# Half of the low part of each weight tile by an adding DMA in place of VectorE, in a one-layer fp32 encoder

## The chip, the cores and the metric

The kernel runs on one core of a Trainium2 chip. The metric is the device time of one execution in microseconds. The core has TensorE (matrix products, into the accumulators called PSUM), VectorE and ScalarE (elementwise work), GpSimd (called POOL in the profile), and 16 DMA engines, to which transfers are sent from the queues of SP, ScalarE or POOL. Each of these engines works through its own list of instructions in order, and they wait for each other by semaphores.

## What is computed

One layer of an encoder on 256 tokens of width 2048, all in fp32: a norm, one input projection to 10,240 columns (queries, keys and values of two kinds of attention, and gates), differential attention and neighbourhood attention, two branch projections that are gated and added, an output projection, a norm with a residual, and a squared-ReLU MLP of width 8192 with a norm and a residual.

```python
h = rms_norm(x, norm_mix_pre[l])
proj = jnp.einsum('bsd,dc->bsc', h, w_in[l])
qa, ka, va, qn, kn, vn, gates = jnp.split(proj, split_at, axis=-1)
...
mixed = (g_a * jnp.einsum('bsc,cd->bsd', oa, w_branch_a[l])
         + g_b * jnp.einsum('bsc,cd->bsd', on, w_branch_b[l]))
y = jnp.einsum('bsd,de->bse', mixed, w_out[l])
x = x + rms_norm(y, norm_mix_post[l])
h = rms_norm(x, norm_mlp_pre[l])
u = jnp.square(jax.nn.relu(jnp.einsum('bsd,df->bsf', h, w_up[l])))
x = x + rms_norm(jnp.einsum('bsf,fd->bsd', u, w_down[l]), norm_mlp_post[l])
```

The weights have 62.9 million numbers (252 MB). Each is read once.

## The kernel before

**Two parts for each number.** TensorE multiplies in a format called float32r, which keeps fewer bits than fp32. So each weight and each activation is given as the sum of a high part (the value cast to float32r) and a low part (value minus high part, again float32r), and a product is made of three: high by high, low by high, high by low.

**Tiles.** Weights come in tiles of 1 MiB, 128 partitions by 2048 numbers. For all projections but the last this is four row blocks of 128 by 512 columns; for the down projection (`dweight`, L750) one row block by 2048 columns. `load` (L94) sends the DMA of a tile into a buffer `raw` from SP's queue (L98). `split` (L101) makes the two parts in the buffers `hi` and `lo`. It does so in two pieces of 128 by 1024 (the very first tile: four pieces): for each, ScalarE casts raw to hi (L115) and VectorE subtracts hi from raw into lo (L116). The pool `wp` has three buffers each of raw, hi and lo, so a load waits until the split of the tile three before is done with its raw buffer, and a split waits until TensorE has used the tile three before.

**Who uses them.** `wgroup` (L183) keeps weights stationary: for four blocks of 128 columns and four row blocks, one product of the high part with both parts of the activations (512 columns, L191) and one of the low part with the high part of the activations (256 columns, L192). `agroup` (L220) and the down projection (`dmm`, L772) keep activations stationary and make three products of 512 columns (L229 to L231, L777 to L779). In `wgroup` and `agroup` the second piece of a tile is its third and fourth row block; in the down projection it is columns 1024 to 2047, used from the third of eight accumulators on.

**Order.** Input projection (20 groups of four tiles, with the stages of the attention heads traced between the tiles by `advance`, L172), in the last part with the branch projections (two tiles a group) among the gates; then the output projection (16 tiles), the MLP's up projection (64), and the down projection (64). The names in the profile follow the projections: `qa`, `ka`, `va`, `qn`, `kn`, `vn` for query, key and value; `ga`, `gb` gates; `ba`, `bb` branches; `y` output; `u` up; `d` down. `u_w`, `u_h`, `u_l` are raw, high and low part of a tile of the up projection; `u_p` its accumulators, `acc` those of the down projection. Besides the tiles, VectorE and ScalarE empty the accumulators (`halves`, L251), and do the norms' and the attention's elementwise work.

**Other lines named below.** `inv_rms` (L81) computes a norm's factor: its power runs on POOL (L88), the only work that POOL has once the constants are made. `residual_parts` (L653) adds the residual (L657) and transposes for the MLP (L664). A chore (L323, L336) prepares the position bias by way of DRAM. The order of each engine's instructions is set by a planner that lays out the traced program in simulated time.

Of the kernel before, what the change touches and what calls it, by code (L numbers as in the profile page):

```python
# [38 lines left out]
def encoder_layer(ctx: ExitStack, tc: tile.TileContext, a, out):  # L39
# [30 lines left out]
        return tmp.tile([P, 2, T], F32, tag="t2k", name=n, bufs=7)  # L70

    def along_tokens(r, b, name):
        """r [P tokens, token tile] as a row of all tokens, on all partitions."""
        ps = bank(f"{name}_p")
        for t in range(2):
            dg = t1k(f"{name}_d{t}")
            nc.vector.tensor_scalar_mul(dg[:, :P], ident, r[:, t : t + 1])
            nc.tensor.matmul(ps[:, t * P : (t + 1) * P], ones, dg[:, :P], start=True, stop=True)
        nc.scalar.copy(b, ps[:, :T])

    def inv_rms(ss, n, name, r=None):  # L81
        """(ss / n + eps) ** -0.5, per partition."""
        w = ss.shape[1]
        ms_ = small(w, f"{name}_m")
        nc.vector.tensor_scalar(ms_, ss, 1.0 / n, EPS, op0=ALU.mult, op1=ALU.add)  # L85
        if r is None:
            r = small(w, f"{name}_r")
        nc.gpsimd.tensor_tensor(r, ms_, expo[:, :w], op=ALU.pow)  # L88
        return r

# [1 line left out]
    last_load = [None]  # L92

    def load(src, k0, nk, c0, cw, name):  # L94
        """Rows k0*128.. of a weight: [P, nk, cw]."""
        raw = wp.tile([P, nk, cw], F32, tag="raw", name=f"{name}_w")
        view = src[k0 * P : (k0 + nk) * P, c0 : c0 + cw].rearrange("(k p) c -> p k c", p=P)
        last_load[0] = nc.sync.dma_start(raw, view).ins  # L98
        return raw

    def split(raw, name, pieces=2, after=()):  # L101
        """Two float32r parts whose sum is raw. after[s] are instructions that go ahead of piece s."""
        _, nk, cw = raw.shape
        hi = wp.tile([P, nk, cw], F32R, tag="hi", name=f"{name}_h")
        lo = wp.tile([P, nk, cw], F32R, tag="lo", name=f"{name}_l")
        for s in range(pieces):
            part = (
                (slice(None), slice(s * nk // pieces, (s + 1) * nk // pieces))
                if nk > 1
                else (slice(None), slice(None), slice(s * cw // pieces, (s + 1) * cw // pieces))  # L110
            )
            with ExitStack() as order:
                for ins in after[s] if after else ():
                    order.enter_context(tc.issue_after(ins))
                nc.scalar.copy(hi[part], raw[part])  # L115
                nc.vector.tensor_sub(lo[part], raw[part], hi[part].bitcast(F32))  # L116
        return hi, lo

    def weight(src, k0, nk, c0, cw, name, after=()):
        return split(load(src, k0, nk, c0, cw, name), name, after=after)  # L120

# [1 line left out]
    g_pre = const.tile([P, KD], F32, name="g_pre")  # L123
    nc.scalar.dma_start(g_pre, a["g_mix_pre"])
    ident = const.tile([P, P], F32, name="ident")
# [44 lines left out]
    pace = [1]  # L170

    def advance(n):  # L172
        """Trace the next n stages of the attention heads that wait for their turn, and one chore."""
        if chores:
            with tc.issue_after(last_load[0]):
                chores.pop(0)()
        for _ in range(n):
            if pending:
                g = pending.pop(0)
                if next(g, None):  # L180
                    pending.append(g)

    def wgroup(src, c0, act, nk, evac, name, first=(), hook=None, mid=None, after={}, k_first=False, inner=None):  # L183
        """out^T of 512 columns: weights stationary. act(k) is [P, hi 256 | lo 256]."""
        ps = [bank(f"{name}_p{b}", True) for b in range(4)]

        def product(b, k, w):
            hi, lo = w
            cs = slice(b * P, (b + 1) * P)
            mv = act(k)  # L190
            nc.tensor.matmul(ps[b], hi[:, k % 4, cs], mv, start=(k == 0), stop=False)  # L191
            nc.tensor.matmul(  # L192
                ps[b][:, :T], lo[:, k % 4, cs], mv[:, :T], start=False, stop=(k == nk - 1)
            )

        for ch in range(nk // 4):
            ks = range(ch * 4, ch * 4 + 4)
            order = hook(ch) if hook else None
            advance(pace[0])
            if ch < len(first):  # L200
                w = split(first[ch], f"{name}_{ch}", 4 if ch == 0 else 2, order)
            else:
                w = weight(src, ch * 4, 4, c0, 512, f"{name}_{ch}", [after.get(ch, ())] * 2)
            if k_first and ch == 0:
                last = None
                for k in ks:
                    last = (inner(k) if inner else None) or last
                    with tc.issue_after(last) if last else nullcontext():
                        for b in range(4):
                            product(b, k, w)  # L210
            else:
                for b in range(4):
                    for k in ks:
                        product(b, k, w)
                    if ch == nk // 4 - 1:
                        if mid and b == 0:
                            mid()
                        evac(b, ps[b])

    def agroup(src, c0, stat, nk, evac, name, tail=1, between=None):  # L220
        """out of 512 columns: activations stationary. stat(k, t) is (hi, lo) of [P, 128].
        The last ``tail`` chunks go token tile by token tile; between(i) may trace instructions
        ahead of the i-th of the second tile's products there and returns the last of them."""
        ps = [bank(f"{name}_p{t}", True) for t in range(2)]

        def product(t, k, w):
            hi, lo = w
            sh, sl = stat(k, t)
            nc.tensor.matmul(ps[t], sh, hi[:, k % 4], start=(k == 0), stop=False)  # L229
            nc.tensor.matmul(ps[t], sh, lo[:, k % 4], start=False, stop=False)  # L230
            nc.tensor.matmul(ps[t], sl, hi[:, k % 4], start=False, stop=(k == nk - 1))  # L231

        n = nk // 4
        for ch in range(n - tail):
            advance(pace[0])
            w = weight(src, ch * 4, 4, c0, 512, f"{name}_{ch}")
            for t in range(2):
                for k in range(ch * 4, ch * 4 + 4):
                    product(t, k, w)
        advance(pace[0])  # L240
        ws = [weight(src, ch * 4, 4, c0, 512, f"{name}_{ch}") for ch in range(n - tail, n)]
        for t in range(2):
            last = None
            for i, k in enumerate(range((n - tail) * 4, nk)):
                if t and between:
                    last = between(i) or last
                with tc.issue_after(last) if last else nullcontext():
                    product(t, k, ws[i // 4])
            evac(t, ps[t])

    def halves(ps, name):  # L251
        """The sum of the two halves of a bank, in SBUF."""
        r = t1k(f"{name}_r")
        nc.scalar.copy(r, ps[:, T:])
        s = t1k(f"{name}_s")
        nc.vector.tensor_add(s, ps[:, :T], r)
        return s

# [1 line left out]
    hT = [page([P, 2, 512], F32R, f"hT{i}") for i in range(8)]  # L260

    def x_parts(i):
        """The transpose of four tiles of x times the gain, in two parts [P, hi | lo]."""
        acts = []
        for k in range(i * 4, i * 4 + 4):
            pt = bank(f"hT_t{k}")
# [50 lines left out]
        )  # L317
        nc.vector.tensor_scalar_mul(subs, subln, 1.0 - LAMBDA_INIT)

    # Position bias: row (h, i) of rpbp holds the bias of row offset i - 3 at column offsets  # L320
    # -63..63. Each is written 64 times at a pitch of 127 and read at a pitch of 126.
    def skew_write(h):
        nc.sync.dma_start(  # L323
            skew[h * NR : (h + 1) * NR].rearrange("r c j -> c r j"),
# [38 lines left out]
            x_squares(3)  # L363
        return [[]] + [acts[i : i + 1] for i in range(3)] if ch == 0 else None

# [1 line left out]
    oT = {}  # L367

    def parts(dst, at, src):
# [2 lines left out]
        nc.vector.tensor_sub(lo[at], src, hi[at].bitcast(F32))  # L372

    def product3(ps, stat, s_at, mov, m_at, start, stop):
        """ps (+)= stat^T @ mov, each given in two parts."""
        for i, (sp, mp) in enumerate(((0, 0), (0, 1), (1, 0))):
            nc.tensor.matmul(
                ps, stat[sp][s_at], mov[mp][m_at], start=start and i == 0, stop=stop and i == 2
# [38 lines left out]
        return evac  # L417

    def p_transposed(p, name):
        """[P queries, (t, keys)] -> [P keys, (key tile, queries)]"""  # L420
        pt = bank(f"{name}_pt")
        for kt in range(2):
            for t in range(2):
# [167 lines left out]
                chores += [lambda: None] * 10 + [partial(position_bias, j) for j in range(2, 4)]  # L591
    pace[0] = 2

# [1 line left out]
    mT = []  # L595
    for cg in range(4):
        gate = []
# [22 lines left out]
        nc.vector.tensor_sub(ml, gate[0], mh.bitcast(F32))  # L620
        mT.append((mh, ml))

# [1 line left out]
    def mstat(k, t):  # L624
        mh, ml = mT[k // 4]
        return mh[:, k % 4, t * P : (t + 1) * P], ml[:, k % 4, t * P : (t + 1) * P]
# [87 lines left out]
    tail = [residual_parts(1, 0)]  # L714
    after = {1: tail[0][1:]}

# [1 line left out]
    def first_up_inner(k):  # L718
        if k == 1:
            tail.append(residual_parts(1, 1, tail[0][2]))  # L720
# [101 lines left out]
def _host_arrays(inputs):  # L822
# [15 lines left out]
        "lam_k1": f["lam_k1"],  # L838
        "lam_q2": f["lam_q2"],
        "lam_k2": f["lam_k2"],  # L840
        # row offsets -3..3 are the ones that four rows reach
        "rpbp": np.pad(f["na_rpb"][0][:, 4:11], ((0, 0), (0, 0), (48, 48))),
    }
    inv = np.float32(1.0) / (
# [28 lines left out]
```

## Time and profile before

| | us |
|---|---|
| median of three runs | 1397.35 |
| lowest and highest | 1396.53, 1397.74 |
| span of the profiled execution, first to last instruction | 1394.5 |
| TensorE / VectorE / ScalarE / POOL busy in it | 1374.6 / 835.8 / 668.7 / 7.9 |
| load queue, share of the 16 DMA engines | 57.3% |

Durations in the profile come from the one profiled execution. A busy TensorE is not one at its peak, since its products overlap and their ends are modelled. Shares of the DMA engines are the time that packets took, over 16 engines and the span; in short windows they can exceed 1 where packets overlap. The mean granted clock of TensorE in this execution is 0.995 of full speed. In rows such as `L115 ACT CAST d_h<-d_w ... x128 | 128.3, 1052 | 191.1 <-PE acc L779 187.5`, the first pair is busy time in us and the mean of one in ns, and what follows is the engine's idle time just before and what ended it.

### The profile page before, as it was taken

What the parts mean: (1) busy time and instruction counts of PE and PEld (TensorE: products, weight loads), DVE (VectorE), ACT (ScalarE), POOL (GpSimd) and SP (SyncE); (2) the same over time, 40 slices, a digit from 0 to 9 for tenths busy, and PEclk for the clock granted to TensorE, in tenths of its full rate; (3) what the DMA queues carried; (4) which work ended last, traced back from release to release, by engine and by line L of the source; (5) the groups of instructions that cost most, each with busy time, mean ns of one, the idle gap of its engine ahead of it and who ended that gap; (6) DMA issues with size and microseconds to landing.
All of it is one profiled execution on the core that took longest, in us unless ns stands there. A gap on an engine that the chain in (4) does not pass through costs nothing.

```text
span 1394.5 us, 17896 instructions
## 1 busy us (share of the span) xinstructions
PE 1374.6 (99%) x7240; PEld 1177.8 (84%) x7240; DVE 835.8 (60%) x1155; ACT 668.7 (48%) x1023; POOL 7.9 (1%) x19
## 2 busy tenths in 40 slices
PE   7999999999999999999899999999999999999997
PEld 6888888888888888888788888888888888888886
DVE  6868866676656565654755555555575554444445
ACT  7554554545444445543744444444464543334332
POOL 0000000000000000000000000000000000000000
PEclk9999999999999999999999999999999999999999
DMA  9674755564555555675455565656555556555551
GB/s 317 202 214 154 202 177 173 171 191 155 165 205 182 203 181 183 203 279 184 149 182 181 182 193 170 211 170 200 189 196 185 203 186 227 195 187 205 181 199 73
DMA packets 117490, 265.16 MB, mean 190 GB/s; under 512 B 15008, under 2 KB 16288, under 8 KB 109216
## 3 DMA queue, kind: packets, MB, share of 16 engines
q1 hardware_dynamic: 117264, 264.03, 57.3%
q8 instruction: 56, 0.92, 0.3%
q14 instruction: 26, 0.21, 0.0%
q10 hardware_dynamic: 144, 0.01, 0.0%
HBM read 261.92 MB, written 3.92 MB: 191 GB/s over the span
## 4 chain that ended last, share of the span: by engine, by line
PE 98%; DVE 1%; DMA 0%; ACT 0%; SPq 0%; issue 0%; DVEq 0%; POOLq 0%; POOL 0%; ACTq 0%
PE u_p L191 17%; PE u_p L192 9%; PE acc L779 8%; PE acc L778 8%; PE acc L777 8%; PE gb_p L191 4%; PE ga_p L191 4%; PE qa_p L191 2%; PE gb_p L192 2%; PE ga_p L192 2%; PE ka_p L191 2%; PE qn_p L191 2%; PE bb_p L191 2%; PE ba_p L191 2%; PE kn_p L191 2%; PE y_p L229 2%
## 5 line engine op out<-in xcount | busy, mean ns | idle before, releaser
L191 PE MATMUL u_p<-h2T,u_h 128*128 128x512 f32 x1024 | 359.9, 398 | 0.5 <-DVE r_m L85 0.5
L192 PE MATMUL u_p<-h2T,u_l 128*128 128x256 f32 x1024 | 284.3, 280 | 0.0
L116 DVE TENSOR_TENSOR d_l<-d_w,d_h 128x1024 fp32r<-128x1024 f32 x128 | 151.1, 1221 | 164.2 <-ACT d_h L115 163.7
L116 DVE TENSOR_TENSOR u_l<-u_w,u_h 128x1024 fp32r<-128x1024 f32 x128 | 151.1, 1222 | 146.0 <-ACT u_h L115 144.7
L191 PEld LDWEIGHTS u_p<-h2T,u_h 128*128 128x128 f32 x1024 | 192.0, 189 | 45.5 <-DVE r_m L85 0.9
L115 ACT CAST d_h<-d_w 128x1024 fp32r<-128x1024 f32 x128 | 128.3, 1052 | 191.1 <-PE acc L779 187.5
L778 PE MATMUL acc<-d_l,uh 128*128 128x512 f32 x512 | 199.0, 389 | 0.0
L779 PE MATMUL acc<-d_h,ul 128*128 128x512 f32 x512 | 198.9, 389 | 0.0
L777 PE MATMUL acc<-d_h,uh 128*128 128x512 f32 x512 | 198.2, 389 | 0.0
L192 PEld LDWEIGHTS u_p<-h2T,u_l 128*128 128x128 f32 x1024 | 193.8, 189 | 1.3
L115 ACT CAST u_h<-u_w 128x1024 fp32r<-128x1024 f32 x128 | 128.0, 1049 | 123.9 <-PE u_p L191 62.5
L778 PEld LDWEIGHTS acc<-d_l,uh 128*128 128x128 f32 x512 | 96.1, 188 | 20.1
L777 PEld LDWEIGHTS acc<-d_h,uh 128*128 128x128 f32 x512 | 96.1, 188 | 20.0
L779 PEld LDWEIGHTS acc<-d_h,ul 128*128 128x128 f32 x512 | 96.1, 188 | 19.8
L191 PE MATMUL gb_p<-hT,gb_h 128*128 128x512 f32 x256 | 90.4, 398 | 0.0
L191 PE MATMUL ga_p<-hT,ga_h 128*128 128x512 f32 x256 | 90.0, 397 | 0.0
L192 PE MATMUL gb_p<-hT,gb_l 128*128 128x256 f32 x256 | 71.4, 281 | 0.0
L192 PE MATMUL ga_p<-hT,ga_l 128*128 128x256 f32 x256 | 70.3, 280 | 0.0
L191 PEld LDWEIGHTS gb_p<-hT,gb_h 128*128 128x128 f32 x256 | 47.9, 188 | 11.5
L116 DVE TENSOR_TENSOR gb_l<-gb_w,gb_h 128x1024 fp32r<-128x1024 f32 x32 | 37.8, 1221 | 31.1 <-ACT gb_h L115 31.1
L191 PEld LDWEIGHTS ga_p<-hT,ga_h 128*128 128x128 f32 x256 | 47.4, 188 | 10.5
L116 DVE TENSOR_TENSOR y_l<-y_w,y_h 128x1024 fp32r<-128x1024 f32 x32 | 37.9, 1222 | 27.8 <-ACT y_h L115 27.8
(213 smaller groups left out, 2348.1 us busy)
## 6 DMA issues: line engine op xcount, KB each, us to landing
u_w<-in_w_up SPq DMA_DIRECT2D x64, 1024.0 KB, 5.4
d_w<-in_w_down SPq DMA_DIRECT2D x64, 1024.0 KB, 4.9
ga_w<-in_w_in SPq DMA_DIRECT2D x16, 1024.0 KB, 5.2
gb_w<-in_w_in SPq DMA_DIRECT2D x16, 1024.0 KB, 5.2
y_w<-in_w_out SPq DMA_DIRECT2D x16, 1024.0 KB, 5.1
ka_w<-in_w_in SPq DMA_DIRECT2D x8, 1024.0 KB, 6.1
va_w<-in_w_in SPq DMA_DIRECT2D x8, 1024.0 KB, 5.2
qn_w<-in_w_in SPq DMA_DIRECT2D x8, 1024.0 KB, 5.1
```

Source lines behind the costliest of these rows:

```text
L115: nc.scalar.copy(hi[part], raw[part])
L116: nc.vector.tensor_sub(lo[part], raw[part], hi[part].bitcast(F32))
L191: nc.tensor.matmul(ps[b], hi[:, k % 4, cs], mv, start=(k == 0), stop=False)
L192: nc.tensor.matmul(ps[b][:, :T], lo[:, k % 4, cs], mv[:, :T], start=False, stop=(k == nk - 1))
L229: nc.tensor.matmul(ps[t], sh, hi[:, k % 4], start=(k == 0), stop=False)
L777: nc.tensor.matmul(acc[t][c], uh[:, k % 4, ts_], hi[:, 0, cs], start=(k == 0), stop=False)
L778: nc.tensor.matmul(acc[t][c], uh[:, k % 4, ts_], lo[:, 0, cs], start=False, stop=False)
L779: nc.tensor.matmul(acc[t][c], ul[:, k % 4, ts_], hi[:, 0, cs], start=False, stop=(k == NK - 1))
```

## The change

For the second of the two pieces of each tile, VectorE's subtraction is replaced. ScalarE writes the negative high part into lo, and an adding DMA, issued from POOL's queue, adds raw onto it in place. The first piece, and the four pieces of the very first tile, are made as before. The other lines of the diff are docstrings and comments that fall away.

```diff
                 nc.scalar.copy(hi[part], raw[part])
-                nc.vector.tensor_sub(lo[part], raw[part], hi[part].bitcast(F32))
+                if s == 1 and pieces == 2:
+                    nc.scalar.mul(lo[part], hi[part].bitcast(F32), -1.0)
+                    nc.gpsimd.dma_start(lo[part], raw[part], accum_op=ALU.add)
+                else:
+                    nc.vector.tensor_sub(lo[part], raw[part], hi[part].bitcast(F32))
```

## The prediction, made before the changed kernel was run

> **What bounds the kernel now.** I read the page first (busy time, chain, DMA queues), then the list of waits, then the order of time in the last stage, and last the windows.
>
> ```profile
> span 1394.5 us, 17896 instructions
> ...
> PE 1374.6 (99%) x7240; PEld 1177.8 (84%) x7240; DVE 835.8 (60%) x1155; ACT 668.7 (48%) x1023; POOL 7.9 (1%) x19
> ...
> q1 hardware_dynamic: 117264, 264.03, 57.3%
> ...
> PE 98%; DVE 1%; DMA 0%; ACT 0%; SPq 0%; issue 0%; DVEq 0%; POOLq 0%; POOL 0%; ACTq 0%
> ```
>
> TensorE is busy 99% of the span, and the chain that ended last is 98% TensorE. VectorE, which the change relieves, works 60% of the span and holds 1% of the chain. All that any relief could bring is the time without TensorE: 1394.5 - 1374.6 = 19.9 us, and most of that is start and end. The DMA engines, which the change loads, are at 57.3% with 264.03 MB.
>
> How a tile moves is seen best in the down projection, in order of time on ScalarE, VectorE and the load queue:
>
> ```profile
> 1200.64 2.01 ACT L115 CAST d_h<-d_w 128x1024 fp32r<-128x1024 f32 x2 [3.43 <-PE acc L779]
> 1206.08 2.00 ACT L115 CAST d_h<-d_w 128x1024 fp32r<-128x1024 f32 x2 [3.43 <-PE acc L779]
> ...
> 1201.73 2.36 DVE L116 TENSOR_TENSOR d_l<-d_w,d_h 128x1024 fp32r<-128x1024 f32 x2 [3.07 <-ACT d_h L115]
> ...
> 1204.11 5.77 SPq L98 DMA_DIRECT2D d_w<-in_w_down  x2
> ...
> d_w<-in_w_down SPq DMA_DIRECT2D x64, 1024.0 KB, 4.9
> ```
>
> One tile takes 1206.08 - 1200.64 = 5.44 us. ScalarE casts only when TensorE has given back a buffer (that of three tiles before), VectorE follows and is done at 1204.09, and at 1204.11 SP sends the load into the raw buffer that VectorE has just finished with. The load lands 4.9 us later, at about 1209. That buffer's next cast comes three tiles after the one at 1200.64, at 1217, so 8 us are to spare. The split itself is ready at 1204.1 for products that begin two tiles after the cast, at about 1211.5. So every producer has room, and TensorE alone sets the pace.
>
> **The change part by part.** A tile is 1 MiB; there are 80 of the input projection, 16 of the branches, 16 of the output, 64 up and 64 down, 240 in all. The first is cut in four and keeps VectorE, so 239 tiles are changed.
>
> ```profile
> L116 DVE TENSOR_TENSOR d_l<-d_w,d_h 128x1024 fp32r<-128x1024 f32 x128 | 151.1, 1221 | 164.2 <-ACT d_h L115 163.7
> ...
> L115 ACT CAST d_h<-d_w 128x1024 fp32r<-128x1024 f32 x128 | 128.3, 1052 | 191.1 <-PE acc L779 187.5
> ...
> 680.00:1030.00 350.00, 350.00 (x2009) 305.28 (x2008) 198.44 (x268) 172.56 (x271) 0.54 (x1) 1.00 0.59 187
> ```
>
> Removed: 239 subtractions of 1221 ns, 292 us of VectorE. Off the path, so worth nothing by itself. Added on ScalarE: 239 multiplications of the shape of the cast, 1052 ns as an estimate from that row, 251 us; ScalarE goes to about 920 us, 66%. In the window of the up projection it is busy 172.56 of 350 us and would be at about 172.56 + 62 x 1.05 = 238; the idle time hides it (without that cover it would be the 251 us). Behind a multiplication in ScalarE's order stand the next tile's casts and the copies out of the accumulators, 1 us later than now; they have the microseconds shown above.
>
> Added on POOL's queue: 239 DMA issues, each of which waits for ScalarE's multiplication. POOL's own price of one isn't in the trace; SP's are these, with other DMAs for what a transfer costs:
>
> ```profile
> L98 SPq DMA_DIRECT2D d_w<-in_w_down x64: 327/328/341, 1012.9 to 1356.4; - x64
> ...
> L336 SPq DMA_DIRECT2D bias<-skew x16: 586/625/1438, 148.4 to 291.6; - x16
> ...
> gpost<-in_g_mix_post SPq DMA_DIRECT2D x2, 512.0 KB, 7.9
> ...
> 670.92 0.55 POOL L88 TENSOR_TENSOR ry<-ry_m,expo 128x1 f32<-128x1 f32 x1 [5.82 <-DVE ry_m L85]
> ```
>
> 0.33 to 1.44 us an issue; I take 1 us, well under 5.4 us, so POOL keeps up. Behind a waiting issue stand the powers of the norms (the last row), on which VectorE's residual and then TensorE wait between output and up projection. At worst each of the few on the path is held for one tile, 5 us; I take 2 us in all.
>
> The term that decides is the **adding DMA's time on the 16 engines**. From the queue's row, 1 MiB costs 0.573 x 1394.5 us / (264.03 / 1.049) = 3.17 us of all 16 engines. An add writes 0.5 MiB, and to do so has to read both raw and the negative high part, 1 MiB of reads. The trace shows no adding DMA and none within SBUF. Low end: charged like a copy of 0.5 MiB, 1.59 us (nothing on the path). High end: the 512 KB row, 7.9 us to landing, less the fixed part of a load (4.9 - 3.17 = 1.7), 6.2 us. Between ends so far apart I take the row that is nearest in what is read, the load of 1 MiB: **3.17 us**. So a tile asks 6.34 us of the engines, more than the 5.44 us that TensorE gives it. The DMA engines become the bound, and a late add also holds back the raw buffer, and so the next load, which now goes at 1204.11; SP works in order, so all later loads stand behind it.
>
> Stage by stage, from the first and last products:
>
> ```profile
> L192 PE MATMUL qa_p<-hT,qa_l x128: 274/281/415, 10.0 to 106.9; 128*128 128x256 f32 x128
> ...
> L192 PE MATMUL ga_p<-hT,ga_l x256: 274/280/370, 305.3 to 535.8; 128*128 128x256 f32 x128
> ...
> L230 PE MATMUL y_p<-y_l,mh x128: 387/389/398, 581.2 to 668.5; 128*128 128x512 f32 x128
> ...
> L192 PE MATMUL u_p<-h2T,u_l x1024: 274/280/415, 674.6 to 1037.1; 128*128 128x256 f32 x171
> ...
> L778 PE MATMUL acc<-d_l,uh x512: 387/389/389, 1037.4 to 1385.0; 128*128 128x512 f32 x171
> ```
>
> Query, key and value: 10.0 to 305.3, 48 tiles, 6.15 us a tile (attention's products lie among them); 6.34 costs 0.19 x 48 = 9. Gates and branches: to 581.2, 48 tiles, 5.75; 0.59 x 48 = 28. Output: to 674.6, 16 tiles, 5.84; 8. Up: to 1037.4, 64 tiles, 5.67; 0.67 x 64 = 43. Down: to 1385.0, 64 tiles, 5.43; 0.91 x 64 = 58. Together 146 us, with POOL's 2 us 148, and the span 1394.5 + 148 = 1542.5. The median of the runs, 1397.35, is 2.85 us above the span; with that **1545 us**.
>
> That assumes engines that never idle. What speaks to that:
>
> ```profile
> 0.00:25.00 25.00, 17.79 (x94) 15.23 (x95) 14.75 (x28) 19.14 (x40) 1.59 (x9) 1.00 0.92 317
> ...
> 1103.00:1104.00 1.00, 1.00 (x6) 0.84 (x5) 0.91 (x2) 1.00 (x2) 0.00 (x0) 1.00 1.08 451
> ...
> 1109.00:1110.00 1.00, 1.00 (x6) 0.81 (x5) 0.62 (x1) 1.00 (x2) 0.00 (x0) 1.00 1.03 434
> ```
>
> At the 0.92 of the first 25 us a tile takes 6.34 / 0.92 = 6.89 us, 0.55 x 240 = 132 us more: 1677. But inside a load the share is 1.03 to 1.08, since packets overlap and their times count first latency too. I keep 1.00, in the middle between this and the next rival. The forecast's own range is 1480, where that rival ends, to 1677.
>
> **Rivals.** *The engines stream faster than the packets' time says.* At the 434 GB/s of the last row, 1.05 MB takes 2.42 us; load and add together are 4.84 us, under 5.44. Then the circle of a raw buffer decides: three ScalarE steps 3.05, POOL 1, an add and a load at 1.7 + 2.4 each: 12.3 us against the 16.3 of three tiles. When both transfers overlap fully it becomes 12.3 + 4.8 = 17.1, 5.7 us a tile. That is 0 to 0.27 us a tile in the down stage, little in the others; with late splits in the up stage, whose copies share ScalarE, I give 40 us: 1435, from 1400 to 1480. For it: those two windows. Against: the mean of all the loads is 3.17.
>
> By the Trainium skill, "DMA: Bandwidth & Descriptors", section "Where 436 GB/s comes from", transfers between SBUF and SBUF are limited at 435 GB/s by the fabric, which would make this rival the outcome, 2.41 us an add with two reads, about 1435 us; this trace agrees in the two single windows (434 and 451) and has no transfer within SBUF. "Collectives: The Full Stack", section "The bandwidth ceiling: the fold count and why AG ≠ RS ≠ AR", says that a reduction by DMA is slow for its two source reads and not for the add; no run here shows it yet.
>
> *The add is charged like a copy of half the size, and all is hidden.* 3.17 + 1.59 = 4.76 us a tile, an add lands within about 1 + 1.7 + 1.6 = 4.3 us, in the clock of the rows above at 1200.64 + 3.05 + 4.3 = 1208, before TensorE asks at 1211.5. Then 1397, no change: the bound was TensorE and stays so.
>
> *The adding is slow in itself* (arithmetic on fp32, cut-up packets, a long issue on POOL). At the high end a tile takes 3.17 + 6.2 = 9.37 us, 240 x 9.37 = 2249 us; I set this case from 1677 to 2260, its middle near 1900. For it: the rows of small and broadcast transfers. Against: runs of 4 KB a partition, the plainest shape here.
>
> *Faster.* A free VectorE shortens the joint between output and up projection:
>
> ```profile
> PE h2T_t L664 <- DVE x L657: 3.2, 1, 3.2
> ...
> 671.50 2.08 DVE x L657 x3
> ```
>
> TensorE waits 3.2 us there for VectorE's residual. If subtractions moved away let it run earlier, 1394 is reached; this needs the add to be hidden, under about 2.2 us of engine time, and POOL not to hold the power in front of it. In these rows no subtraction stands in VectorE's way there, so little speaks for it.
>
> **How the numbers follow.** Forecast, 1480 to 1677: 0.35. Streaming engines, 1400 to 1480: 0.20. Hidden, no change: 0.15. Slow add to 2100: 0.19; beyond: 0.07. Faster by more: 0.04. The range 1396 to 2100 leaves out 0.07, 0.04 and a part of the hidden case, under 0.2. A measurement of this kernel tells about 0.2% (2.8 us) from no change: faster 0.04, same 0.15, slower 0.81.
>
> **What would show it.** Right: VectorE near 544 us, ScalarE near 920; a new DMA queue from POOL with 239 issues of 512 KB; the DMA share over 90% in the up and down windows; TensorE waiting at the products with u_l and d_l for a DMA; landing of an add near 5 us or more and of a load well above 4.9. The stages should lose in the order down, up, gates, with query/key/value least. Wrong: an add of under 2 us of engine time (TensorE stays at 99%, time unchanged), or over 4 us (every stage at the same step per tile, attention's stage too). Also wrong if ScalarE or POOL shows no idle time, or if the waits fall at the joints and not in the tiles.

## The result and the profile after

The changed kernel takes 1566.8 us (median of 4 runs, 1560.7 to 1571.6) against 1397.6 us before: ratio 1.121, 95% interval 1.120 to 1.123, 12.1% slower. The forecast was 1545. The profiled execution has a span of 1565.4 us, 171 us more than before. First the page of the changed kernel: span, busy times, DMA queues (packets, MB, share of the 16 engines), and the chain that ended last.

```profile
span 1565.4 us, 19169 instructions
...
PE 1430.9 (91%) x7240; PEld 1201.3 (77%) x7240; DVE 575.6 (37%) x916; ACT 900.0 (57%) x1262; POOL 215.7 (14%) x258
...
q1 hardware_dynamic: 117264, 264.03, 50.8%
q0 software_dynamic: 34416, 125.32, 42.7%
...
DMA 52%; PE 21%; issue 15%; ACT 8%; DVE 2%; SPq 1%; POOL 0%; POOLq 0%; ACTq 0%; DVEq 0%
```

TensorE's idle time rose from 19.9 to 134.5 us, and the same 7240 products are busy 56 us longer. The mean granted clock fell from 0.995 to 0.971, so (1 - 0.971) x 1565 = 45 us of full speed are missing, against 7 us before. That is at most 38 of the 56 us. The chain that was 98% TensorE is now 52% DMA. The new queue q0 holds the adds: 125 MB written, 42.7% of the engines' time. The two queues together fill 93.5% by their packets. VectorE has lost its 239 subtractions, and nothing of that shows in the time.

Who waits for the adds: from the lists of waits (us in total, times, longest), TensorE's and SP's, and from the page the adds' issue on POOL and their time to landing.

```profile
PE u_p L196 <- DMA u_l<-u_w: 26.4, 18, 3.5
PE acc L782 <- DMA d_l<-d_w: 25.2, 14, 4.1
...
SPq L98 <- DMA u_l<-u_w: 383.8, 64, 19.3
SPq L98 <- DMA d_l<-d_w: 341.6, 61, 10.9
...
L118 POOL DMA_DIRECT2D d_l<-d_w x64 | 55.8, 872 | 331.7 <-ACT d_l L117 253.0
...
d_w<-in_w_down SPq DMA_DIRECT2D x64, 1024.0 KB, 7.0
u_l<-u_w POOLq DMA_DIRECT2D x64, 512.0 KB, 8.3
d_l<-d_w POOLq DMA_DIRECT2D x64, 512.0 KB, 6.7
```

Two waits are new. TensorE waits for low parts, as the up and down rows show. And every load of the up projection (64 of 64), and nearly every one of the down projection, now waits in SP's queue for an add to land. Before, it was mostly VectorE that a load waited for, as the longest row of the same list of the kernel before shows:

```profile
SPq L98 <- DVE d_l L116: 290.0, 59, 9.1
```

POOL is not the bound: 0.87 us an issue, 14% busy.

The chain in order of time in the down projection (start, us, what) shows the second wait as a circle:

```profile
1300.37 6.09 DMA d_l<-d_w
...
1306.60 9.48 DMA d_w<-in_w_down
...
1316.14 3.41 issue
...
1319.56 8.87 DMA d_l<-d_w
```

An add lands after 6.09 us; only then does the load into that raw buffer go, and it takes 9.48 us, where a load took 4.9 before; ScalarE's three steps and POOL's wake-up take 3.41; then comes the add of that buffer's next tile. From add to add it is 1319.56 - 1300.37 = 19.2 us for three tiles (there are three raw buffers), 6.4 us a tile, where TensorE needs 5.43. This is one turn; over the whole stage it is 388.9 / 64 = 6.08 us a tile.

TensorE waits for that last add to land. What follows is seen in its product (the wait stands in the brackets) and in windows of 2 us (the first two numbers are TensorE's busy time and products, the third from the end its granted clock):

```profile
1328.47 0.79 PE L782 MATMUL acc<-d_l,uh 128*128 128x512 f32 x1 [4.11 <-DMA d_l<-d_w]
...
1320.00:1322.00 2.00, 2.00 (x11) 1.65 (x10) 0.00 (x0) 0.72 (x1) 0.43 (x1) 1.00 0.86 227
...
1330.00:1332.00 2.00, 2.00 (x6) 1.56 (x5) 0.62 (x1) 1.37 (x2) 0.30 (x1) 0.50 0.98 365
1332.00:1334.00 2.00, 2.00 (x6) 1.57 (x5) 0.00 (x0) 0.00 (x0) 0.57 (x1) 0.50 1.02 397
1334.00:1336.00 2.00, 2.00 (x8) 1.58 (x8) 0.00 (x0) 0.45 (x1) 0.00 (x0) 0.83 0.99 283
1336.00:1338.00 2.00, 2.00 (x10) 1.65 (x9) 1.23 (x1) 1.97 (x3) 0.00 (x0) 1.00 0.95 213
```

After the wait of 4.11 us the clock stands at 0.50 for some 6 us, in which TensorE starts six products in 2 us instead of eleven. So this wait cost about 3 us (half of the 6) more than its own length.

By stage, from the first and last products with a low part (durations, then first and last start):

```profile
L196 PE MATMUL qa_p<-hT,qa_l x128: 274/280/415, 10.5 to 118.8; 128*128 128x256 f32 x128
L196 PE MATMUL ga_p<-hT,ga_l x256: 274/280/386, 328.9 to 585.7; 128*128 128x256 f32 x128
L234 PE MATMUL y_p<-y_l,mh x128: 387/389/795, 638.3 to 751.0; 128*128 128x512 f32 x128
L196 PE MATMUL u_p<-h2T,u_l x1024: 274/280/583, 757.0 to 1165.2; 128*128 128x256 f32 x171
L782 PE MATMUL acc<-d_l,uh x512: 387/389/796, 1165.5 to 1554.4; 128*128 128x512 f32 x171
```

| stage | before, us | after, us | more | forecast |
|---|---|---|---|---|
| query, key, value | 295.3 | 318.4 | 23 | 9 |
| gates and branches | 275.9 | 309.4 | 34 | 28 |
| output | 93.4 | 118.7 | 25 | 8 |
| up | 362.8 | 408.5 | 46 | 43 |
| down | 347.6 | 388.9 | 41 | 58 |

Every stage loses, the output stage most per tile. The time from the last such product of the output stage to the first of the up stage hardly changed (6.1 us before, 6.0 after), so the loss lies in the tiles and not in that joint.

### The profile page after: what moved, and what is told of

It reads as the page before. It is cut to its first block, busy times and chain, and to the rows that moved or that the text cites. A ratio compares the mean times of both kernels' runs of the same rounds, so it can differ in the third digit from the quotient of the medians.

```text
span 1565.4 us, 19169 instructions
## 1 busy us (share of the span) xinstructions
PE 1430.9 (91%) x7240; PEld 1201.3 (77%) x7240; DVE 575.6 (37%) x916; ACT 900.0 (57%) x1262; POOL 215.7 (14%) x258
## 3 DMA queue, kind: packets, MB, share of 16 engines
q0 software_dynamic: 34416, 125.32, 42.7%
## 4 chain that ended last, share of the span: by engine, by line
DMA 52%; PE 21%; issue 15%; ACT 8%; DVE 2%; SPq 1%; POOL 0%; POOLq 0%; ACTq 0%; DVEq 0%
DMA u_w<-in_w_up 9%; DMA u_l<-u_w 8%; DMA d_w<-in_w_down 7%; DMA d_l<-d_w 7%; DMA y_w<-in_w_out 3%; PE ga_p L195 2%; PE u_p L195 2%; DMA ka_w<-in_w_in 2%; PE acc L782 2%; PE acc L783 2%; PE bb_p L195 2%; PE acc L781 2%; DMA ga_l<-ga_w 2%; PE gb_p L195 2%; DMA qn_w<-in_w_in 2%
## 5 line engine op out<-in xcount | busy, mean ns | idle before, releaser
L196 PEld LDWEIGHTS u_p<-h2T,u_l 128*128 128x128 f32 x1024 | 197.4, 193 | 39.2 <-DMA u_l<-u_w 33.2
L782 PE MATMUL acc<-d_l,uh 128*128 128x512 f32 x512 | 203.5, 402 | 25.5 <-DMA d_l<-d_w 25.2
L781 PE MATMUL acc<-d_h,uh 128*128 128x512 f32 x512 | 185.8, 397 | 0.0
L120 DVE TENSOR_TENSOR d_l<-d_w,d_h 128x1024 fp32r<-128x1024 f32 x64 | 78.4, 1225 | 275.4 <-ACT d_h L115 275.4
L120 DVE TENSOR_TENSOR u_l<-u_w,u_h 128x1024 fp32r<-128x1024 f32 x64 | 78.4, 1225 | 239.6 <-ACT u_h L115 239.6
L118 POOL DMA_DIRECT2D u_l<-u_w x64 | 55.8, 872 | 343.9 <-ACT u_l L117 207.9
L118 POOL DMA_DIRECT2D d_l<-d_w x64 | 55.8, 872 | 331.7 <-ACT d_l L117 253.0
L196 PE MATMUL gb_p<-hT,gb_l 128*128 128x256 f32 x256 | 68.1, 282 | 3.5 <-DMA gb_l<-gb_w 3.5
L117 ACT ACTIVATE d_l<-d_h 128x1024 fp32r<-128x1024 f32 x64 | 67.7, 1060 | 1.7
L117 ACT ACTIVATE u_l<-u_h 128x1024 fp32r<-128x1024 f32 x64 | 67.7, 1058 | 1.5
```

Source lines behind the costliest of these rows:

```text
L117: nc.scalar.mul(lo[part], hi[part].bitcast(F32), -1.0)
L118: nc.gpsimd.dma_start(lo[part], raw[part], accum_op=ALU.add)
L196: nc.tensor.matmul(ps[b][:, :T], lo[:, k % 4, cs], mv[:, :T], start=False, stop=(k == nk - 1))
L781: nc.tensor.matmul(acc[t][c], uh[:, k % 4, ts_], hi[:, 0, cs], start=(k == 0), stop=False)
L782: nc.tensor.matmul(acc[t][c], uh[:, k % 4, ts_], lo[:, 0, cs], start=False, stop=False)
```

## The experiments

Four theories stood at the start. **A**: a load and an add ask more of the 16 DMA engines than a tile of TensorE's work leaves (3.16 us a load and 0.427 x 1565.4 / 239 = 2.80 us an add by their packets, 5.96 us together). **B**: raw is held until the add lands, so loads go late. **C**: TensorE waits for a late low part. **D**: ScalarE's third step, or the planner's order with it. The kernel before ran beside each group, at 1396.9 to 1397.9 us. The short diffs are against the changed kernel.

**VectorE instead of the DMA** (`e_vec`).

```diff
-                    nc.gpsimd.dma_start(lo[part], raw[part], accum_op=ALU.add)
+                    nc.vector.tensor_add(lo[part], raw[part], lo[part].bitcast(F32))
```

> ScalarE writes the negative high part as in the changed kernel, and VectorE adds raw onto it; no adding DMA. Theory A (the 16 DMA engines: a load of 3.16 us and an add of 2.80 us per tile leave too little time), theory B (the raw buffer is held until the add has landed, so loads go late) and theory C (TensorE waits for a low part that lands late, engines have time to spare) all expect 1397 to 1401 us. Theory D (ScalarE's third step, or the order that the planner makes with it) expects over 1420 us.

1400.3 us, ratio 1.0024 (1.0014 to 1.0033). ScalarE is at 900 us as in the changed kernel, and the time is 3 us above that of before. Theory D falls: the adding DMA makes the loss, not the step that prepares it.

**The add reads the high part** (`e_src`).

```diff
-                    nc.gpsimd.dma_start(lo[part], raw[part], accum_op=ALU.add)
+                    nc.gpsimd.dma_start(lo[part], hi[part].bitcast(F32), accum_op=ALU.add)
```

> The adding DMA reads the high part instead of raw, so raw is given back as early as before, with the same bytes moved and the same wait of TensorE for the low part (the low part of the second piece becomes zero). Theory A: still 1530 to 1570 us. Theory B: 1397 to 1430 us. Theory C: 1500 to 1570 us, with TensorE's waits for the low part as now and loads landing on time.

1485.8 us, ratio 1.065 (1.062 to 1.067). Outside all three ranges, between A's and B's: giving raw back early is worth 81 us of the 169, and the rest stays. (The high part is now what the add holds.) The queues of its page, and its DMA issues:

```profile
q1 hardware_dynamic: 117264, 264.03, 53.0%
q0 software_dynamic: 34416, 125.32, 42.9%
...
u_w<-in_w_up SPq DMA_DIRECT2D x64, 1024.0 KB, 10.3
d_l<-d_h POOLq DMA_DIRECT2D x64, 512.0 KB, 9.5
```

The engines are 95.9% full by packets, and each transfer in these two projections lands later than in the changed kernel (a load of the up projection in 10.3 us instead of 6.6). That more of them are under way at once would explain it; this was not tested.

**Adds that nobody waits for** (`e_free`, against the kernel before; the lines that make the two scratch buffers and the smaller pools are left out).

```diff
+                if s == 1 and pieces == 2:
+                    hs = hi[part].bitcast(F32).rearrange("p k c -> p (k c)")
+                    for i in range(2):
+                        nc.gpsimd.dma_start(scratch[i], hs[:, i * 512 : (i + 1) * 512], accum_op=ALU.add)
```

> VectorE makes both low parts as before the change, ScalarE has no third step; beside it two adding DMAs of 256 KB a tile add the high part onto two scratch buffers that nobody reads. Same bytes as in the changed kernel, no wait of TensorE for them and raw not held; temporary buffers one fewer of each kind. Theory A: 1500 to 1570 us. Theories B, C and D: 1397 to 1410 us.

1611.5 us, ratio 1.153 (1.150 to 1.156): above every range, and nearest to theory A's. But its list of waits shows that it tested something else:

```profile
POOL scratch L123 <- DMA scratch<-d_h: 270.6, 90, 6.8
...
ACT d_h L118 <- DMA scratch<-d_h: 244.6, 57, 8.9
```

Each add onto a scratch buffer had to wait for the last one there to land, and it held its high part meanwhile, so ScalarE's casts waited for the adds. The experiment had made a circle of its own. It decides nothing between A and B.

**A copy instead of an add** (`e_copy`).

```diff
-                    nc.gpsimd.dma_start(lo[part], raw[part], accum_op=ALU.add)
+                    nc.gpsimd.dma_start(lo[part].bitcast(F32), raw[part])
```

> As the changed kernel, but the DMA copies raw over the low part instead of adding it (the low part of the second piece is then raw itself). Same issue, same waits, one read instead of two. Theory A: an engine time of about 1.4 to 1.6 us, 4.7 us a tile, so 1397 to 1410 us. Theories B and C: landing falls from 7 to about 4.5 us, 1397 to 1430 us. If what costs is the issue on POOL and the fixed time of its DMAs, 1500 us or more.

1420.9 us, ratio 1.018 (1.016 to 1.019): in the range of B and C, above A's.

```profile
q0 software_dynamic: 34416, 125.32, 22.6%
```

A copy of 512 KB takes 0.226 x 1417.4 (its span) / 239 = 1.34 us of the engines, an add of the same size 2.80. The prediction had counted two reads for one write; the ratio of 2.1 bears that out. It also agrees with what the Trainium skill says in "Collectives: The Full Stack", section "The bandwidth ceiling: the fold count and why AG ≠ RS ≠ AR": that the second source read, not the addition, is what a reducing DMA pays for. The run doesn't part A from B: a copy takes less of the engines and also lands sooner (4.8 us in the down projection instead of 6.7).

**The second piece first** (`e_first`).

```diff
-        for s in range(pieces):
+        for s in (range(pieces) if pieces > 2 else (1, 0)):
```

> As the changed kernel, but the second piece goes first: ScalarE casts and negates it and the add is issued, then the first piece follows. Same bytes; the add starts about 1 us earlier after the load has landed, and raw is given back as much earlier. If the engines' time alone counts (5.96 us a tile): 1560 to 1572 us. If the time for which raw is held counts as well: 1500 to 1550 us.

1584.3 us, ratio 1.132 (1.127 to 1.137): outside both ranges. ScalarE and POOL in order of time show why:

```profile
1300.35 2.00 ACT L115 CAST d_h<-d_w 128x1024 fp32r<-128x1024 f32 x2 [1.59 <-DMA d_w<-in_w_down]
1302.24 1.06 ACT L117 ACTIVATE d_l<-d_h 128x1024 fp32r<-128x1024 f32 x1
...
1303.60 0.87 POOL L118 DMA_DIRECT2D d_l<-d_w  x1 [3.68 <-DVE d_l L120]
```

The planner put both casts ahead of the negation again. In this tile the add goes 3.25 us after the first cast, against 3.39 in the tile of the chain above (1316.17 to 1319.56), so an add that starts 1 us earlier was not tried by this. The add's wait here ends with VectorE's subtraction of the other piece. Where the 17 us more come from stays open.

**Raw held and the bytes moved, but no wait of TensorE** (`e_hold`).

```diff
+                nc.vector.tensor_sub(lo[part], raw[part], hi[part].bitcast(F32))
                 if s == 1 and pieces == 2:
-                    nc.scalar.mul(lo[part], hi[part].bitcast(F32), -1.0)
-                    nc.gpsimd.dma_start(lo[part], raw[part], accum_op=ALU.add)
-                else:
-                    nc.vector.tensor_sub(lo[part], raw[part], hi[part].bitcast(F32))
+                    nc.gpsimd.dma_start(raw[part], hi[part].bitcast(F32), accum_op=ALU.add)
```

> VectorE makes both low parts as before the change and ScalarE has no third step; then an adding DMA adds the high part onto the raw piece that is done with. Same bytes, raw held until the add has landed, but TensorE waits for no add. If TensorE's wait for a late low part is needed for the loss: 1400 to 1490 us. If engines' time and the held raw buffer make it: 1540 to 1575 us.

1557.0 us, ratio 1.114 (1.111 to 1.118), in the range of A with B. With three raw buffers TensorE's own wait for the low part costs little: without it the time is 10 us less, though the two TensorE rows of the changed kernel's list show 51.6 us of it. TensorE is then idle for 1551.6 - 1428.5 = 123 us on other waits.

**Half the dose**, in each tile (`e_half`) or in every second tile (`e_alt`).

```diff
+                    if nk > 1:
+                        p1, p2 = (slice(None), slice(2, 3)), (slice(None), slice(3, 4))
+                    else:
+                        p1, p2 = [(slice(None), slice(None), slice(c, c + 512)) for c in (1024, 1536)]
+                    nc.scalar.mul(lo[p2], hi[p2].bitcast(F32), -1.0)
+                    nc.gpsimd.dma_start(lo[p2], raw[p2], accum_op=ALU.add)
+                    nc.vector.tensor_sub(lo[p1], raw[p1], hi[p1].bitcast(F32))
```

```diff
+        turn[0] += 1
         for s in range(pieces):
...
-                if s == 1 and pieces == 2:
+                if s == 1 and pieces == 2 and turn[0] % 2:
```

> Half the dose in each tile: VectorE makes half of the second piece as before, ScalarE and the adding DMA the other half (256 KB an add, 239 adds). Engines' time by theory A: 3.16 + 1.40 = 4.56 us a tile, under TensorE's 5.43 to 6.15: 1397 to 1415 us. If a fixed time of each adding DMA counts rather than its bytes: 1480 to 1570 us.

> Half the dose by leaving out every second add: 119 tiles as in the changed kernel, the others with VectorE alone. Engines' time by theory A on average 4.56 us a tile, so 1397 to 1420 us; if each added tile costs its share whatever its neighbours do, half of the loss, about 1480 us.

`e_half` 1414.0 us, ratio 1.012 (1.010 to 1.014), as A expected. `e_alt` 1427.8 us (1418.7 to 1436.7), ratio 1.022 (1.016 to 1.028), 8 us above A's range and far from the 1480 of a price per add. Half of the dose costs a tenth or a fifth of the loss, not half. In `e_half` the same 239 DMAs are issued, so no fixed price of a DMA makes the loss. But this doesn't part A from B: in `e_half` the adds also land sooner (4.7 us in the down projection), and in `e_alt`, where they land no sooner (8.4 us), only every second tile holds its raw buffer for one.

**A fourth raw buffer.** It needs room, so both kernels have one page fewer and one temporary buffer fewer of each kind; `e_small` with three raw buffers is the one to compare with.

```diff
-        raw = wp.tile([P, nk, cw], F32, tag="raw", name=f"{name}_w")
+        raw = wp.tile([P, nk, cw], F32, tag="raw", name=f"{name}_w", bufs=4)
```

> The changed kernel with 26 pages in place of 27 and one temporary buffer fewer of each kind, three raw buffers: what the next kernel gives up for its room. All theories: as the changed kernel, 1560 to 1590 us.

> The changed kernel with a fourth raw buffer (and the smaller pools of the run beside it). Loads no longer wait for the add of three tiles before. If half the loss is the held raw buffer: 1475 to 1510 us, like the kernel whose add reads the high part. If the engines' time is all: 1555 to 1590 us.

`e_small` 1583.2 us, ratio 1.134 (1.130 to 1.137). `e_raw4` 1498.1 us, ratio 1.073 (1.066 to 1.079), in the range of the held buffer: 85 us of the loss are gone with one buffer. What is left is seen in its ScalarE, POOL, chain and TensorE in the down projection, and in its list of waits:

```profile
1306.94 2.00 ACT L115 CAST d_h<-d_w 128x1024 fp32r<-128x1024 f32 x2 [2.34 <-PE acc L783]
...
1310.33 0.87 POOL L118 DMA_DIRECT2D d_l<-d_w  x1 [4.57 <-ACT d_l L117]
...
1310.33 9.45 DMA d_l<-d_w
...
1319.82 0.50 PE L782 MATMUL acc<-d_l,uh 128*128 128x512 f32 x1 [0.45 <-DMA d_l<-d_w]
...
PE u_p L196 <- DMA u_l<-u_w: 30.4, 22, 3.8
PE acc L782 <- DMA d_l<-d_w: 13.9, 11, 3.7
```

ScalarE waits for TensorE again and no longer for a load. From the cast to the add's landing it is 3.39 + 9.45 = 12.84 us. TensorE reaches the second piece two tiles and six products later, 2 x 5.44 + 6 x 0.23 = 12.3 us. So the low part is some 0.6 us late by this sum, and TensorE waits 0.45 us for it. Most tiles of the down projection show no such wait (11 times in 64 tiles), but some wait up to 3.7 us. This is theory C, and it shows once B is out of the way.

**Four raw buffers and no wait of TensorE** (`e_hold4`: the edit of `e_hold` in `e_raw4`). ScalarE's third step goes with it, which `e_vec` puts at 3 us.

> Four raw buffers, and the add of the high part onto the raw piece that is done with, VectorE making both low parts: same bytes, TensorE waits for no add, the raw buffer's delay has room. If the rest of the loss is the engines' time (5.8 us a tile against 5.4 to 5.8): 1470 to 1500 us. If it is TensorE's wait for a late low part: 1397 to 1420 us.

1422.6 us, ratio 1.017 (1.014 to 1.020), 3 us above the range of C (1397 to 1420) and far from A's. From its page and its windows (the first is the stretch; PE, PEld, DVE, ACT, POOL; the last three granted clock, DMA share, GB/s):

```profile
span 1419.5 us, 18564 instructions
...
q1 hardware_dynamic: 117264, 264.03, 54.2%
q0 software_dynamic: 34416, 125.32, 45.7%
...
700.00:1000.00 300.00, 298.94 (x1713) 260.54 (x1712) 165.10 (x221) 145.46 (x228) 46.05 (x54) 1.00 1.03 277
```

All of the changed kernel's bytes are moved, by engines that are 99.9% busy by packets, in a kernel 25 us slower than before. So the bytes alone cost no more than that; the engines' time is just about enough. By subtraction, the other 140 us and more of the loss come from waiting on late transfers, with the slower clock after the waits.

**Both pieces by adds** (`e_double`: `if pieces == 2:` in place of `if s == 1 and pieces == 2:`).

> Both pieces of each tile by ScalarE's negation and an adding DMA: two adds of 512 KB a tile. If the engines' time sets the end: 3.16 + 2 x 2.80 = 8.76 us a tile, 2100 us, with some loss for held buffers 2100 to 2250. If the wait for one add's landing sets it (two adds in flight together): 1600 to 1800 us.

2020.5 us, ratio 1.449 (1.440 to 1.457): outside both ranges, below A's 2100 and far above the 1800 of a wait for landing.

```profile
span 2012.7 us, 19122 instructions
...
q0 software_dynamic: 68832, 250.64, 65.7%
q1 hardware_dynamic: 117264, 264.03, 36.1%
```

By packets the engines are at 101.8%. Against `e_hold4`, at 99.9%, 239 adds more cost (2012.7 - 1419.5) / 239 = 2.48 us each. This is an estimate: it takes both kernels to be at their engines' limit, and `e_double` has late transfers and a clock of 0.908 besides.

## Why the prediction was right in its number, and where its steps were off

*What bounded the kernel, VectorE's relief, ScalarE, POOL.* Right. VectorE's freed time brought nothing; it came to 576 us and not to 544, and nothing hangs on that. ScalarE rose to 900 us (920 forecast) and hid it, as `e_vec` shows; a POOL issue is 0.87 us (1 taken).

*The adding DMA's time, "the load of 1 MiB: 3.17 us".* Right in kind, too high in size. An add takes 2.1 times a copy's time (`e_copy`), as two reads would. By packets it is 2.80 us, and 2.48 us by the estimate from `e_double`. Reading 1.05 MB in 2.48 us is 423 GB/s, which is the rival of streaming engines (2.42 us), and close to the 435 GB/s for transfers within SBUF of the Trainium skill, "DMA: Bandwidth & Descriptors", section "Where 436 GB/s comes from". The two windows that the prediction held beside that limit (434 and 451 GB/s) show loads from DRAM, and one of them lies above it, so they don't bear it out.

*"The DMA engines become the bound."* This is the step that failed in the main, though the number came out. The prediction got its 146 us from engines that are asked for too much, and "assumes engines that never idle". With nearly full engines and little waiting, the same bytes cost 25 us (`e_hold4`). With the measured prices the prediction's own sum by stages gives 67 us (2.80 us an add, 5.97 a tile) or 14 us (2.48, 5.65 a tile), not 146. And in the changed kernel the engines did idle, by packets 6.5% of a longer span.

*"A late add also holds back the raw buffer."* Named, and given no price of its own beside the engines' time. It had the largest: a fourth raw buffer takes off 85 us (1583 to 1498), a source other than raw 81 us (1567 to 1486). The circle of three raw buffers, put at 12.3 to 17.1 us in the rival, was 19.2 us in the chain, since a load takes 9.5 us and an add 6 to 9 when they overlap. The second wait, TensorE's for the low part, is worth 75 us where raw has four buffers (1498 to 1423) and 10 us where it has three (1567 to 1557). Seen the other way, where TensorE waits for no add a fourth raw buffer takes off 134 us (1557 to 1423, with the smaller pools on one side only). So the parts don't add up one by one. It looks as if the later of the two waits counts, and as if both grow with the traffic that they share; no run shows this by itself.

*The number.* The engines' time was put at 146 us where at most 25 were found; the two waits, about 140 us, had no price. The two errors nearly cancel. The direction followed from the DMA work that the change adds; how near 1545 comes to 1567 is luck.

*By stage.* The order forecast was down, up, gates, and little elsewhere. Up, down and gates lost most, but query/key/value lost 23 us instead of 9 and output 25 instead of 8. At the measured 5.96 us a tile, prices of engine time alone would give nothing in the query stage, which has 6.15 us a tile before and 318.4 / 48 = 6.63 after. A fourth raw buffer (`e_raw4` against `e_small`) takes the query stage's loss from 27 to 15 us and the output stage's from 25 to 10, so a good part of both is the held buffer. Why the circle is longest in the output stage (7.4 us a tile) stays open.

*The signs.* Those named for "right" came true: a share over 90% in the up and down windows, TensorE's waits at `u_l` and `d_l`, later landings. They fit a held buffer as well as full engines, so they could not tell the two apart.

*Open.* `e_hold4` has the smaller pools, which cost the changed kernel 16 us; what bytes alone cost with the old pools was not tried. Nor was an add that starts right after its cast. The lower clock is at most 38 us of the loss; it goes with the waits, and no run had the waits without it.

## What to carry to other kernels

Where the matrix engine is 99% busy, work taken off an engine that is 60% busy has nothing to bring, and what it is moved to can cost far more. Before moving elementwise work to an adding DMA, count its reads twice, and follow the circle of every buffer that it reads or writes: issue, landing under load, and what may start only then, against tiles in flight times the time of one tile. When engines look full, take the waits away while all the bytes stay; here that told a full engine from a late transfer, and the share of busy time didn't.

## What the runs showed that was not expected

Transfers that overlap land later: a 1 MiB load of the up and down projections landed after 5.4 and 4.9 us before, and after 6.6 and 7.0 us beside the adds, up to 10.3 us in `e_src`. A share of the DMA engines near 94% doesn't say that the bytes need that span: the changed kernel took 1565 us at 93.5%, and the same bytes went through in 1419.5 us at 99.9%. And TensorE's granted clock sank with its waits: 0.995 before, 0.971 after, 0.908 with both pieces added by DMA. In the trace a wait of 4.11 us was followed by some 6 us at half the clock.
